# Copies of the first activation chunk at another address, and small products of zeros in the down stages

## The chip, the cores and the metric

The kernel runs on one core of a Trainium2 chip. The metric is device time in microseconds (us) of one execution; a kernel's time is the median of its runs. The engines are TensorE (PE, with its weight loads as PEld), VectorE (DVE), ScalarE (ACT), GpSimd (POOL) and SyncE (SP), which issues the DMAs.

## What is computed

A trunk of two layers on 256 tokens of 1024 channels in float32. Each layer is a half-weighted SwiGLU block, a token mixer (stick-breaking attention in layer 0, an RG-LRU recurrent block in layer 1) and another SwiGLU block; each is normalised, scaled and shifted by a conditioning vector, and added to x through a gate.

```
def sublayer_input(x, g, mod_j):
    shift, scale, gate = mod_j[:, 0], mod_j[:, 1], mod_j[:, 2]
    h = rmsnorm(x, g) * (1 + scale[:, None, :]) + shift[:, None, :]
    return h, (1 + gate)[:, None, :]

def swiglu(h, w_gu, w_down):
    g, u = jnp.split(h @ w_gu, 2, axis=-1)
    return (jax.nn.silu(g) * u) @ w_down

# per layer:  x = x + 0.5 * gate * swiglu(h);  x = x + gate * mixer(h);  x = x + 0.5 * gate * swiglu(h)
```

The feed-forward width is 2816, that of the recurrent block 1280.

## The kernel before

The activations stand transposed, channels on the partitions: x is eight chunks (d or k = 0 to 7) of 128 channels x 256 tokens. All large products are of float32 values split in two float32r parts, a high one (wh, and the first tile of a pair hx or arenar) and the rest (wl, and the second). One step of a product is three matmuls of 128 x 128 weights with 128 x 256 moving values, high by high, high by rest and rest by high; they are issued on line 540, in Acc.group.

Weights come by DMA in pieces of 1 MiB (raw, three buffers), ScalarE makes the high part (L511, fh in load) and VectorE the rest (L514, fl). The rings wh and wl have seven tiles each of 128 x 1024.

A sub-layer has an up stage and a down stage. In the up stage of a feed-forward block there are 22 tiles (f = 0 to 21) of two column blocks (gate and up) each; one tile takes eight chunks k of the normalised input, two halves g and three passes, 48 products in all, into one bank of PSUM. In up, chunk k is read from hx_[k], a pair of tiles of the ring hx (20 places, 384 floats apart, 256 or 258 of them used). After it, swiglu_tile makes the result and splits it into a pair in the arena (arenar). The down stage multiplies these with wdn, eight output chunks d by 22 steps, 528 products; its accumulators are five banks. The residual is added at its end (L674), with the squares for the next norm (L609), and scaled makes a first input for the next sub-layer that isn't divided by the root mean square yet (hx, L632 and L634, 258 columns: the last two carry the shift).

With this input the first two tiles of the next sub-layer (NFIRST) are computed in up_first, while norm and norm_chunk make the final input chunk by chunk (VectorE hpre L642, ScalarE hx L490, VectorE hx L644); the tiles from the third on read that. I call this passage a hand-over; there are five. The very first sub-layer has none: its first eight tiles are computed chunk by chunk together (eight wide chunks of 48 products each), and the tiles f = 8 to 21 follow as usual.

The order is not that of the code. Each operation is handed to Program with an engine, a cost and its buffers; schedule works out due times, simulates the engines with these costs, and issues in the order of the simulated starts. A matmul's cost comes from c_mm, that of a step of three products of 256 columns being 3 x 117.8 ns. The rows of modw (144 pieces, products with cact at L572 on VectorE) are handed out by hook along the way; all DMAs are on SP's queue.

Two tiles only shift addresses: pad0 (HXPAD, 112 floats) ahead of the ring hx and pad1 (ARPAD, 16 floats) ahead of the arena.

Of the kernel before, what the change touches and what calls it, by code (L numbers as in the profile page):

```python
# [14 lines left out]
P = 128  # L15
T = 256
# [16 lines left out]
NFIRST = 2  # L33
LAT0 = 950.0
SMALL = (0, 7)
HXPAD, ARPAD = 112, 16

OFF_NG = 0
OFF_MB = OFF_NG + 6 * KD
# [315 lines left out]


def c_mm(n, passes=3):
    return (432.0 if passes == 4 else 117.8 * passes) * max(n, 256) / 256


def c_dma(n):
# [4 lines left out]
def trunk(ctx, tc, xT, cb, par, modw, gu0, gu, wdn, qk, wv, wo, win, wri, wout, out):  # L366
# [24 lines left out]
    whr, _ = ring("wh", 7, HALF, F32R)  # L391
    wlr, _ = ring("wl", 7, HALF, F32R)
    const.tile([P, HXPAD], F32, tag="pad0", name="pad0")
    hxr, _ = ring("hx", 20, TX, F32R, pitch=384)
    sqr, _ = ring("sq", 2, T)
    ssqr, _ = ring("ssq", 2, T)
    rmsr, _ = ring("rms", 1, T)
# [41 lines left out]
    def fixed(name, cols, dt=F32):  # L439
        return const.tile([P, cols], dt, tag=name, name=name)  # L440
# [14 lines left out]
    none_ = fixed("none", P, F32R)  # L455
    dve.tensor_copy(none_, t32[:, P:])
    ident = fixed("ident", P, BF16)
    mask = fixed("mask", T, BF16)
    pool.affine_select(at[1][:, :P], ones, [[1, P]], ALU.is_equal, 0.0, base=0, channel_multiplier=-1)
    dve.tensor_copy(ident, at[1][:, :P])  # L460
# [132 lines left out]
            V(lambda: dve.tensor_scalar(fo(), mi(), 1.0, wt, ALU.add, ALU.mult), n, rr, ww)  # L593


    ssq, hcur, gcur = {}, {}, {}

    def add_square(gen, d):
        if d == 0:
# [47 lines left out]
    def norm(gen, q):  # L647
        for d in range(KD):
            norm_chunk(gen, d, q)

    def down(l, s, nxt, srcs, ys, nlast, hook=None, post=None, n32=0):


        accs = [Acc(f"acc_{l}_{s}_{i}") for i in range(5)]
        place = [(accs[d // 2], d % 2) for d in range(7)] + [(accs[4], 0)]
        gate = mfin[l, s, 2]
        n = len(srcs)
        ws = []

        def step(d, k):  # L660
            acc, j = place[d]
            y, yc = ys(k)
            o = lambda b: b[:, j * T : (j + 1) * T]
            if k < 2 * n32:
                c0 = (k % 2) * D + d * P
                group32(acc, j, o, ws[k], lambda u: u[:, c0 : c0 + P], y, lambda v: v[:, yc], T, False)
            else:
                group(acc, j, o, ws[k], lambda u: u[:, d * P : (d + 1) * P], y, lambda v: v[:, yc], T, k == 2 * n - 1)

        def residual(d):  # L670
            acc, j = place[d]

            def fn():
                dve.scalar_tensor_tensor(x[d](), acc.b()[:, j * T : (j + 1) * T], gate()[:, d : d + 1], x[d](), ALU.mult,  # L674
                                         ALU.add)
            V(fn, T, [(acc.b, j), (gate, d), x[d]], [x[d]], ptr=1)
            add_square(nxt, d)
            if nxt != "end":
                scaled(nxt, d)
            else:  # L680
                A(x[d], x[d], AF.Copy, T, [x[d], pars], [x[d]], ptr=1, scale=lambda: col(OFF_FG + d))

        for c in range(n):
            if c < n32:
                raw = Buf(rawr)
                dma(raw, srcs[c], CH, [raw])
                ws += [raw, raw]
            else:
                ws += load(srcs[c], CH, f"dn_{l}_{s}_{c}")
            if hook is not None:  # L690
                hook(c)
            if c < n - nlast:
                for d in range(KD):
                    for k in (2 * c, 2 * c + 1):
                        step(d, k)
            if post is not None:
                post(c)
        for ds in ((0, 1), (2, 3), (4, 5), (6,), (7,)):
            for d in ds:
                for k in range(2 * (n - nlast), 2 * n):  # L700
                    step(d, k)
            for d in ds:
                residual(d)

    def up(acc, ws, hx_):

        for k in range(KD):
            for g in range(2):
                c0 = (k % 4) * 256 + g * P
                group(acc, (g, 0), lambda b, g=g: b[:, g * T : (g + 1) * T], ws[k // 4],  # L710
                      lambda u, c0=c0: u[:, c0 : c0 + P], hx_[k], lambda v: v[:, :T], T, k == KD - 1)

    def up_first(gen, ws, scale=(1.0, 1.0)):

# [35 lines left out]
    def ffn(l, s, nxt, hook):  # L750
# [8 lines left out]
        if j == 0:  # L759
# [32 lines left out]
                              lambda u, c0=c0: u[:, c0 : c0 + P], hcur[0, 0][k], lambda v: v[:, :T], T, k == KD - 1)  # L792
            for f in range(SQ):
                swiglu_tile(accs[f], tile_out())
        else:
            f0 = NFIRST

# [8 lines left out]
        for f in range(f0, NF):  # L806
            hook(f)
            acc = Acc(f"g_{j}_{f}")
            up(acc, load(gu[j, f], CH, f"gu_{j}_{f}", chained if j == 0 and f == f0 else None), hcur[l, s])
            swiglu_tile(acc, tile_out())  # L810
        down(l, s, nxt, [wdn[j, :, 2 * c : 2 * c + 2, :].rearrange("p k d -> p (k d)") for c in range(NF // 2)],
             lambda k: (ys[k], slice(0, T)), 2, lambda c: hook(NF + 2 * c))
# [2 lines left out]
    def attention(l, s, nxt, hook):  # L815
# [45 lines left out]
        def q_proj(f):  # L861
# [11 lines left out]
                    put(g, *v)  # L873
                return
            acc = Acc(f"qk{f}")
            up(acc, q_load(f), hcur[l, s])

            def put2(g, scale):
                b, rd = acc.b, (acc.b, (g, 0))
# [115 lines left out]
        def tail(c):  # L995
# [3 lines left out]
            if c == 1:  # L999
                values(7)  # L1000

        down(l, s, nxt, [wo[:, 2 * c : 2 * c + 2, :].rearrange("p k d -> p (k d)") for c in range(4)],
             lambda k: (os_[k], slice(0, T)), 2, lambda c: hook(8 + c), tail)


    def rglru(l, s, nxt):
# [47 lines left out]
        def xb_proj(n2):  # L1054
# [7 lines left out]
                    A(lambda: xb()[:, 4:], t, AF.Identity, T, [t, rd], [xb], ptr=1, bias=c)  # L1062
            else:
                acc = Acc(f"xb{n2}")
                up(acc, load(win[1, n2], CH, f"xb{n2}"), hcur[l, s])

                def evict(e, xb):
                    A(lambda: xb()[:, 4:], lambda: acc.b()[:, e * T : (e + 1) * T], AF.Copy, T, [(acc.b, (e, 0))], [xb],
# [3 lines left out]

        def gate_proj(n2):
            acc = Acc(f"gt{n2}")
            up(acc, load(win[0, n2], CH, f"gt{n2}"), hcur[l, s])
            b = acc.b
            g = gt[n2] = Buf(F, 4)
            A(g, b, AF.Copy, 2 * T, [(b, (0, 0)), (b, (1, 0))], [g], psum=True)
# [51 lines left out]
        for n2 in range(NB):  # L1130
            output(n2)
        down(l, s, nxt, [wout[:, 2 * c : 2 * c + 2, :].rearrange("p k d -> p (k d)") for c in range(NB)],
             lambda k: ys[k], 2, n32=N32)

    def final():
        q = rstd("end")
# [146 lines left out]
```

## Time and profile before

| | us |
|---|---|
| median of 3 runs | 970.75 |
| lowest, highest | 966.33, 980.56 |
| profiled execution, its own time | 976.08 |
| its span in the trace | 974.3 |

The profile is one execution. A group's row gives the union of its busy times, then the mean length of one record. Records of products overlap, as products are pipelined: a record lasts longer than the time to the next one's start. Line 490 is the helper that issues all of ScalarE's activations, so its groups go by tiles.

### The profile page before, as it was taken

The page shows a single profiled execution, that of the slowest core. Times are in us where ns is not written, and L with a number is a line of the kernel's source. Part 1 is how long each engine was busy: PE and PEld are TensorE (multiplying, and loading weights), DVE is VectorE, ACT ScalarE, POOL GpSimd, SP SyncE. Part 2 cuts the span into 40 slices and gives each one's busy share as a digit, 9 for nine tenths or more (in the row PEclk, how much of TensorE's full clock was granted, in tenths as well). Part 3 has the DMA queues.
Part 4 walks back from the last instruction along what each step waited for, and adds up shares of the span by engine and source line. Part 5 has one row for each costly group of instructions (what it writes and reads, how often), then busy time and mean ns, then how long its engine had stood idle before and what let it go on. Part 6 is the DMA issues. An engine that isn't in the chain of part 4 may idle for free.

```text
span 974.3 us, 19720 instructions
## 1 busy us (share of the span) xinstructions
PE 958.5 (98%) x8096; PEld 946.5 (97%) x8096; DVE 795.5 (82%) x1316; ACT 561.0 (58%) x902; POOL 2.2 (0%) x14
## 2 busy tenths in 40 slices
PE   7999999999999999999999999999999999999997
PEld 5999999999999999999999999999999999999996
DVE  7998988898998999999899999544997997555533
ACT  5475444378886854554366444443869785444333
POOL 0000000000000000000000000000000000000000
PEclk9999999999999999999999999999999999999999
DMA  9989999954775499999976999555424737555531
GB/s 340 364 316 352 350 360 348 350 187 174 250 250 206 142 364 360 363 363 384 345 284 248 348 359 352 214 174 182 164 93 168 258 132 260 178 212 179 173 125 44
DMA packets 48332, 251.25 MB, mean 258 GB/s; under 512 B 5489, under 2 KB 6129, under 8 KB 28530
## 3 DMA queue, kind: packets, MB, share of 16 engines
q1 hardware_dynamic: 48242, 249.99, 69.8%
q8 instruction: 63, 1.03, 0.4%
q14 instruction: 27, 0.22, 0.1%
HBM read 248.92 MB, written 1.05 MB: 257 GB/s over the span
## 4 chain that ended last, share of the span: by engine, by line
PE 79%; DVE 9%; DMA 8%; issue 2%; ACT 1%; SPq 0%; DVEq 0%
PE bank L540 72%; DMA rawm<-in_modw 8%; DVE wl L514 3%; DVE rawm L572 2%; PE bank L844 2%; PE bank L1041 1%; PE bank L967 1%; PE bank L557 1%; PE bank L920 1%; DVE hx L644 1%; PE bank L945 1%; DMA raw<-in_gu 1%; DVE hpre L642 1%; PE bank L1184 0%; DVE arenar L748 0%
## 5 line engine op out<-in xcount | busy, mean ns | idle before, releaser
L540 PE MATMUL bank<-hx,wh 128*128 128x256 f32 (+1 forms) x3392 | 598.0, 280 | 3.6 <-ACT hx L490 2.5
L540 PEld LDWEIGHTS bank<-hx,wh 128*128 128x128 f32 x3392 | 520.3, 189 | 7.0 <-ACT hx L490 3.3
L511 ACT ACTIVATE wh<-raw 128x1024 fp32r<-128x1024 f32 (+1 forms) x328 | 336.8, 1045 | 295.5 <-PE bank L540 211.3
L514 DVE TENSOR_TENSOR wl<-raw,wh 128x1024 fp32r<-128x1024 f32 (+1 forms) x328 | 388.5, 1206 | 116.2 <-ACT wh L511 114.8
L540 PE MATMUL bank<-hx,wl 128*128 128x256 f32 (+1 forms) x1696 | 473.6, 279 | 0.0
L540 PEld LDWEIGHTS bank<-hx,wl 128*128 128x128 f32 x1696 | 319.6, 188 | 0.0
L540 PE MATMUL bank<-arenar,wh 128*128 128x256 f32 x1664 | 289.7, 279 | 0.0
L540 PEld LDWEIGHTS bank<-arenar,wh 128*128 128x128 f32 x1664 | 253.7, 189 | 0.1
L540 PE MATMUL bank<-arenar,wl 128*128 128x256 f32 x832 | 231.8, 279 | 0.0
L572 DVE SCALAR_TENSOR_TENSOR rawm<-rawm,cact 128x1024 f32<-128x1024 f32 x144 | 174.9, 1219 | 21.6 <-DMA rawm<-in_modw 20.9
L540 PEld LDWEIGHTS bank<-arenar,wl 128*128 128x128 f32 x832 | 156.5, 188 | 0.0
L490 ACT ACTIVATE arenar<-a 128x256 fp32r<-128x256 f32 x88 | 35.4, 407 | 18.7 <-DVE a L743 14.3
L748 DVE TENSOR_TENSOR arenar<-a,arenar 128x256 fp32r<-128x256 f32 x88 | 36.3, 417 | 1.2 <-ACT arenar L490 1.2
L490 ACT ACTIVATE sg<-bank 128x256 f32<-128x256 f32 x82 | 29.9, 367 | 8.2 <-PE bank L540 8.2
L743 DVE TENSOR_TENSOR a<-bank,sg 128x256 f32<-128x256 f32 x82 | 33.9, 416 | 0.2
L490 ACT ACTIVATE hx<-hpre,mf 128x256 fp32r<-128x256 f32 x48 | 23.3, 501 | 17.3 <-DVE mf L585 13.4
L490 ACT ACTIVATE hx<-x,mf 128x256 fp32r<-128x256 f32 x40 | 18.6, 502 | 23.7 <-DVE x L674 23.7
L674 DVE SCALAR_TENSOR_TENSOR x<-bank,mf,x 128x256 f32<-128x256 f32 x48 | 21.5, 477 | 8.2 <-PE bank L540 8.2
L844 PE MATMUL bank<-wh,hx 128*128 128x256 f32 x128 | 23.2, 279 | 0.0
L642 DVE SCALAR_TENSOR_TENSOR hpre<-x,mf,rst 128x256 f32<-128x256 f32 x48 | 22.0, 479 | 0.9 <-ACT rst L490 0.4
L644 DVE SCALAR_TENSOR_TENSOR hx<-hpre,mf,hx 128x256 fp32r<-128x256 f32 x48 | 22.7, 478 | 0.0
L490 ACT ACTIVATE arenaf<-arenaf 128x768 f32<-128x768 f32 (+1 forms) x31 | 22.0, 738 | 0.4
(97 smaller groups left out, 448.6 us busy)
## 6 DMA issues: line engine op xcount, KB each, us to landing
raw<-in_gu SPq DMA_DIRECT2D x79, 1024.0 KB, 6.1
rawm<-in_modw SPq DMA_DIRECT2D x144, 512.0 KB, 6.3
raw<-in_wdn SPq DMA_DIRECT2D x44, 1024.0 KB, 6.0
raw<-in_win SPq DMA_DIRECT2D x10, 1024.0 KB, 4.8
raw<-in_qk SPq DMA_DIRECT2D x8, 1024.0 KB, 4.8
raw<-in_gu SPq DMA_DIRECT2D x14, 512.0 KB, 5.9
raw<-in_wout SPq DMA_DIRECT2D x5, 1024.0 KB, 5.0
raw<-in_wv SPq DMA_DIRECT2D x4, 1024.0 KB, 5.8
```

The source lines that it names most:

```text
L490: act.activation(o(), i(), f, **{k: (v() if callable(v) else v) for k, v in kw.items()})
L511: act.activation(h()[:, :m], raw()[:, a : a + m], AF.Copy)
L514: dve.tensor_tensor(lo()[:, :m], raw()[:, a : a + m], f32(h()[:, :m]), ALU.subtract)
L540: pe.matmul(o(b()), wc(u()), xc(v()), start=start and n == 0, stop=stop and n == len(passes) - 1, skip_group_check=True)
L557: pr.op("PE", c_mm(n, 4), lambda: pe.matmul(o(b()), wc(w()), xc(x32()), start=start, stop=stop, skip_group_check=True), [w, x32] + ([] if ...
L572: dve.scalar_tensor_tensor(raw(), raw(), 1.0, cact(), ALU.mult, ALU.mult, accum_out=m()[:, t : t + 1])
L642: V(lambda: dve.scalar_tensor_tensor(hp(), x[d](), gs()[:, c], q(), ALU.mult, ALU.mult), T, [x[d], (gs, d), q], [hp], ptr=1)
L644: V(lambda: dve.scalar_tensor_tensor(lo()[:, :T], hp(), sh()[:, c], f32(hi()[:, :T]), ALU.add, ALU.subtract), T, [hp, (sh, d), hi], [lo], ...
L674: dve.scalar_tensor_tensor(x[d](), acc.b()[:, j * T : (j + 1) * T], gate()[:, d : d + 1], x[d](), ALU.mult, ALU.add)
L743: V(lambda: dve.tensor_tensor(a(), b()[:, T:], sg(), ALU.mult), T, [(b, (1, 0)), sg], [a])
L748: V(lambda: dve.tensor_tensor(y[1](), a(), f32(y[0]()), ALU.subtract), n, [a, y[0]], [y[1]])
L844: pe.matmul(o, u()[:, tb * P : (tb + 1) * P], v()[:, c0 : c0 + 256], start=start and n == 0, stop=k == KD - 1 and n == 2, skip_group_check ...
```

## The change

The tiles of hx lie 320 floats apart instead of 384. A new ring hk holds two tiles of 256 columns behind a pad of 16 floats. At the end of norm (and after the wide tiles of the first sub-layer) other_copy copies both parts of chunk 0 into it, the high part on ScalarE and the rest on VectorE. An up tile with kick set reads chunk 0 from these copies and the other seven from hx as before. Kicked are the feed-forward tiles f in 2, 3, 7, 9, 11, 15, 19 (where the tile is computed by up), all qk tiles from the third on, and all xb and gate tiles of the recurrent block that go through up.

In each down stage, at one of its pieces (the first; in the attention and the recurrent block the second), a product of zeros by 64 columns of the identity, in bf16, is added to the first output chunk's accumulator behind that chunk's first step there. ARPAD becomes 64. The planner's cost of a product becomes 114.0 for 117.8.

```diff
-HXPAD, ARPAD = 112, 16
+HXPAD, HKPAD, ARPAD = 112, 16, 64
+KICKS = (2, 3, 7, 9, 11, 15, 19)
...
-    return (432.0 if passes == 4 else 117.8 * passes) * max(n, 256) / 256
+    return (432.0 if passes == 4 else 114.0 * passes) * max(n, 256) / 256
...
-    hxr, _ = ring("hx", 20, TX, F32R, pitch=384)
+    hxr, _ = ring("hx", 20, TX, F32R, pitch=320)
+    const.tile([P, HKPAD], F32, tag="pad2", name="pad2")
+    hkr, _ = ring("hk", 2, T, F32R)
...
+    zero = fixed("zero", P, BF16)
+    pool.memset(zero, 0.0)
...
     def norm(gen, q):
         for d in range(KD):
             norm_chunk(gen, d, q)
+        other_copy(gen)
+
+    def other_copy(gen):
+        hi, lo = hcur[gen][0]
+        h2, l2 = hkick[gen] = Buf(hkr), Buf(hkr)
+        A(h2, lambda: f32(hi()[:, :T]), AF.Copy, T, [hi], [h2])
+        V(lambda: dve.tensor_copy(l2(), f32(lo()[:, :T])), T, [lo], [l2])
...
-    def down(l, s, nxt, srcs, ys, nlast, hook=None, post=None, n32=0):
+    def down(l, s, nxt, srcs, ys, nlast, hook=None, post=None, n32=0, kicks=(0,)):
...
                     for k in (2 * c, 2 * c + 1):
                         step(d, k)
+                        if d == 0 and k == 2 * c and c in kicks:
+                            kick_op(*place[d])
...
-    def up(acc, ws, hx_):
+    def up(acc, ws, gen, kick=False):
...
+                h = hkick[gen] if kick and k == 0 and gen in hkick else hcur[gen][k]
                 group(acc, (g, 0), lambda b, g=g: b[:, g * T : (g + 1) * T], ws[k // 4],
-                      lambda u, c0=c0: u[:, c0 : c0 + P], hx_[k], lambda v: v[:, :T], T, k == KD - 1)
+                      lambda u, c0=c0: u[:, c0 : c0 + P], h, lambda v: v[:, :T], T, k == KD - 1)
+
+    def kick_op(acc, j):
+
+        b = acc.b
+        pr.op("PE", 130.0, lambda: pe.matmul(b()[:, j * T : j * T + 64], zero, ident[:, :64], start=False, stop=False,
+                                             skip_group_check=True), [(b, "start")], [(b, j)])
...
+            other_copy((0, 0))
...
-            up(acc, load(gu[j, f], CH, f"gu_{j}_{f}", chained if j == 0 and f == f0 else None), hcur[l, s])
+            up(acc, load(gu[j, f], CH, f"gu_{j}_{f}", chained if j == 0 and f == f0 else None), (l, s), f in KICKS)
...
-            up(acc, q_load(f), hcur[l, s])
+            up(acc, q_load(f), (l, s), True)
...
-             lambda k: (os_[k], slice(0, T)), 2, lambda c: hook(8 + c), tail)
+             lambda k: (os_[k], slice(0, T)), 2, lambda c: hook(8 + c), tail, kicks=(1,))
...
-                up(acc, load(win[1, n2], CH, f"xb{n2}"), hcur[l, s])
+                up(acc, load(win[1, n2], CH, f"xb{n2}"), (l, s), True)
...
-            up(acc, load(win[0, n2], CH, f"gt{n2}"), hcur[l, s])
+            up(acc, load(win[0, n2], CH, f"gt{n2}"), (l, s), True)
...
-             lambda k: ys[k], 2, n32=N32)
+             lambda k: ys[k], 2, n32=N32, kicks=(N32,))
```

## Rows read from the trace of the kernel before

**Rows 1.** The page: busy times, granted clock in 40 slices, chain by line.

```profile
PE 958.5 (98%) x8096; PEld 946.5 (97%) x8096; DVE 795.5 (82%) x1316; ACT 561.0 (58%) x902; POOL 2.2 (0%) x14
...
PEclk9999999999999999999999999999999999999999
...
PE bank L540 72%; DMA rawm<-in_modw 8%; DVE wl L514 3%; DVE rawm L572 2%; PE bank L844 2%; PE bank L1041 1%; PE bank L967 1%; PE bank L557 1%; PE bank L920 1%; DVE hx L644 1%; PE bank L945 1%; DMA raw<-in_gu 1%; DVE hpre L642 1%; PE bank L1184 0%; DVE arenar L748 0%
```

**Rows 2.** Windows: from:to, length, busy and (records) per engine; clock, DMA share, GB/s.

```profile
49.60:201.80 152.20, 152.20 (x1294) 152.20 (x1294) 135.37 (x218) 76.35 (x121) 0.00 (x0) 1.00 0.93 343
515.90:689.00 173.10, 173.10 (x1472) 173.10 (x1471) 128.62 (x199) 82.67 (x127) 0.00 (x0) 1.00 0.71 260
709.10:714.30 5.20, 5.20 (x46) 5.20 (x46) 5.13 (x11) 3.94 (x9) 0.00 (x0) 1.00 0.00 0
...
732.80:754.90 22.10, 22.10 (x190) 22.10 (x189) 16.04 (x29) 21.97 (x39) 0.00 (x0) 1.00 0.39 146
762.30:784.50 22.20, 22.20 (x191) 22.20 (x190) 20.38 (x40) 14.99 (x31) 0.00 (x0) 1.00 0.67 242
229.30:234.00 4.70, 4.70 (x42) 4.70 (x42) 4.05 (x7) 3.96 (x6) 0.00 (x0) 1.00 0.90 317
```

**Rows 3.** Windows of two other feed-forward stages and of one tile of 258 columns.

```profile
335.80:499.80 164.00, 164.00 (x1449) 164.00 (x1448) 150.84 (x238) 79.92 (x119) 0.00 (x0) 1.00 0.93 353
797.20:964.90 167.70, 167.70 (x1482) 167.70 (x1481) 93.40 (x128) 79.18 (x117) 0.00 (x0) 1.00 0.47 165
...
791.30:796.70 5.40, 5.40 (x47) 5.40 (x46) 5.40 (x12) 5.34 (x9) 0.00 (x0) 1.00 1.00 401
```

**Rows 4.** Groups by line, 50 to 200 us and 340 to 498 us.

```profile
L540 PE MATMUL bank<-hx,wh 128*128 128x256 f32 x509 | 90.0, 281 | 0.0
...
L540 PE MATMUL bank<-hx,wh 128*128 128x256 f32 x590 | 100.3, 276 | 0.0
```

**Rows 5.** The chain that ended last, in order of time: start, length, what.

```profile
48.92 0.41 DVE hx L644
49.37 158.59 PE bank L540 x1343
```

**Rows 6.** Timeline of TensorE near 796.6 us: start, length, line, operands, form, count.

```profile
796.58 0.28 PE L540 MATMUL bank<-hx,wl 128*128 128x258 f32 x1
796.70 0.41 PE L540 MATMUL bank<-hx,wh 128*128 128x256 f32 x2
```

**Rows 7.** Groups by line, forms apart, whole span: nearest operations and counts.

```profile
L540 PE MATMUL bank<-hx,wh 128*128 128x256 f32 x3072 | 538.6, 280 | 3.2 <-ACT hx L490 2.5 <-DVE hx L644 0.2
L540 PE MATMUL bank<-hx,wl 128*128 128x256 f32 x1536 | 428.2, 279 | 0.0
...
L490 ACT ACTIVATE arenar<-a 128x256 fp32r<-128x256 f32 x88 | 35.4, 407 | 18.7 <-DVE a L743 14.3 <-DVE a L801 4.4
...
L644 DVE SCALAR_TENSOR_TENSOR hx<-hpre,mf,hx 128x256 fp32r<-128x256 f32 x48 | 22.7, 478 | 0.0
L642 DVE SCALAR_TENSOR_TENSOR hpre<-x,mf,rst 128x256 f32<-128x256 f32 x48 | 22.0, 479 | 0.9 <-ACT rst L490 0.4
...
L465 DVE CAST mask<-a 128x256 bf16<-128x256 f32 x1 | 0.3, 294 | 0.4 <-POOL xb L467 0.4
...
L908 PE MATMUL bank<-mask,ident 128*128 128x256 bf16 x16 | 3.1, 278 | 0.0
...
L947 PE MATMUL bank<-arenar,none 128*128 128x128 f32 x32 | 5.3, 248 | 0.0
```

**Rows 8.** Windows of two hand-overs.

```profile
201.90:214.00 12.10, 12.10 (x101) 12.04 (x100) 11.43 (x27) 10.80 (x24) 0.00 (x0) 1.00 0.62 212
...
499.80:515.70 15.90, 15.07 (x118) 14.26 (x116) 15.72 (x34) 14.29 (x25) 0.00 (x0) 1.00 0.61 233
```

**Rows 9.** Waits of 340 to 498 us and 498 to 518 us: us, times, longest.

```profile
ACT wh L511 <- PE bank L540: 54.6, 32, 3.4
...
PEld bank L540 <- DVE hx L644: 0.9, 3, 0.4
```

## What is predicted, and from what

> **What bounds the kernel now.** I began with the page: TensorE is busy for 98% of the span, its granted clock shows the top digit in every slice, and the chain that ended last runs for 72% through one line, L540, the three products of a split matmul [rows 1]. So the end is set by how closely products follow each other, and a change is worth something only if it alters that spacing or stops TensorE.
>
> The busy time does not tell the spacing, since records overlap. The windows do: a window of length w holds (w + one record's length) / spacing products. In two of the four feed-forward stages this gives (152.2 + 0.281) us / 1294 = 117.8 ns and (173.1 + 0.281) / 1472 = 117.8 ns [rows 2]; in the other two (164.0 + 0.276) / 1449 = 113.4 and (167.7 + 0.276) / 1482 = 113.3 ns [rows 3]; the lengths of one record, 281 and 276 ns, differ in the same sense [rows 4]. [...] I call them the 118 and the 113 pace. Vector and scalar engine are not the cause: in the 113 stage from 340 us the scalar engine still waits 54.6 us for TensorE to free weight tiles [rows 9].
>
> What picks the pace? A stretch at 118 begins at 49.37 us, after TensorE had waited for a late chunk, hx from L644 [rows 5]. The stretch at 113 from 797.2 us begins without any wait: 258-column products at about (5.4 + 0.283) / 47 = 121 ns give way directly to 256-column ones, and these run at 113 [rows 3, 6]. There are three such turns from 258 to 256 columns without a wait (the other two near 331 and 701 us), and all three ended at 113. So a wait can end at the slow pace, while slower products just ahead, without a wait, ended at the quick one. This is what I build on; three cases are thin.
>
> The profiled execution took 976.08 us by the clock, 5.3 us above the median of 970.75. One feed-forward stage at the other pace is 1470 x 4.45 ns = 6.5 us, so the spread of the three runs (14.2 us) looks like two stages that fell differently; the sum below is made against 976.08, and what it saves is a draw that the median run had partly won already.
>
> **The change part by part.**
>
> Addresses. Counted in the order of the allocations (2,048 bytes of scratch, four 32-byte constants, then tiles of whole 512 bytes) the weight tiles begin 128 bytes past a multiple of 512, hx and the arena 64 bytes past one (HXPAD 112 and ARPAD 16 floats). After it, hx steps by 1,280 bytes, so it lies at 64 and 320 in turn (64 still, modulo 256); hk, behind 25,600 bytes and a pad of 64, lies at 128; the arena stays at 64. No row has moving data at 320, nor moving data and weights both at 128: what these products cost is bounded by the three spacings seen, 113.3, 117.8 and 121.
>
> Gain. An up tile that is kicked has six products (k = 0, two halves, three passes) on hk, and then returns to hx. If that acts as the 258-column products did, the rest of the tile runs at 113, and so do the tiles behind it. What is at 118 now, behind a first kick:
> - first feed-forward stage: 1294 products, of which 528 are down (11 chunks x 48) and 766 up, 16 tiles of 48. The first kick is f = 9, so 3 x 48 go off, two wide chunks' and f = 8: 1150 x 4.45 ns = 5.1 us [rows 2].
> - third one: kicked from f = 2, 1472 x 4.45 = 6.55 us [rows 2].
> - attention: two qk tiles like the one at 229.3 us, 2 x 42 x 4.45 = 0.4 us [rows 2].
> - recurrent block: two tiles like the one at 709.1, the 190 from 732.8, the 191 down from 762.3: (92 + 381) x 4.45 = 2.1 us [rows 2].
>
> Together 14.1 us. The two stages at 113 stay as they are.
>
> Copies. Six generations, each with a ScalarE copy of 256 columns (0.41 us, as arenar<-a) and a VectorE copy (between the 0.29 of a cast to 256 columns and the 0.48 of L644) [rows 7]. The first stage's pair has a whole tile to finish in: nothing. The other five stand in the hand-over between two sub-layers, where hx is made chunk by chunk and TensorE uses a chunk in 6 x 0.113 = 0.68 us while VectorE needs 2 x 0.48 (L642 and L644) [rows 7]. In the hand-over at 499.8 the weight loads waited for L644 three times [rows 9]. The first kicked product waits for hk, and all products of its tile are queued behind it; the copies in turn stand ahead of later chunks. Between 0 (VectorE moves a weight subtraction back instead) and 5 x (0.41 + 0.48) = 4.5 us; I take one copy exposed each time, 2.0 us, since one hand-over shows such waits and the one at 201.9 none to speak of.
>
> Kicked products. 4 tiles in the first stage, 7 in each of the other three, 6 qk tiles, 3 xb and 5 gate tiles: 39 x 6 = 234. At 113 they cost nothing more, at 121 they cost 234 x 7.6 = 1.8 us; I take the 118 pace, 1.0 us.
>
> Small bf16 products, one in each of six down stages: 64 columns. Nearest are L947 (128 columns, a record of 0.248 us) and L908 (256 columns of bf16, 0.278 us) [rows 7]; a whole record is the upper end, 6 x 0.28 = 1.7 us, the lower 0. I take 0.1 each, 0.6 us. What they do to the pace is a rival below.
>
> Quicker stages elsewhere. The hand-over after the 113 stage took 15.9 us for 118 products, the one after the first 118 stage 12.1 for 101 [rows 8]: at 12.1 / 101 = 0.120 the 118 would have taken 14.1, so 1.8 us were lost to a VectorE that had fallen behind. A quicker first stage, as full of transfers as the second, may lose the same: 0 to 1.8, I take 0.9. The third stage is not as full (DMA share 0.71 against 0.93) [rows 2, 3]: nothing.
>
> New durations (114.0 for 117.8 per product) change only the planner's order. They can move a weight subtraction past a modulation product or back. No row shows the new order; the 1.8 us of one hand-over bounds it either way, taken as 0. The memset on POOL lies before the first product.
>
> Sum: 976.1 - 14.1 + 2.0 + 1.0 + 0.6 + 0.9 = **966.5 us**. With all unknowns at their lower ends it is 962.0, with the upper ends 971.8; the order moves either by 1.8.
>
> [...] The two paces at one clock show that something does hold products back, but no row shows that it is the address.
>
> **The rivals.**
> *The kick does nothing, or only draws again.* For it: the pace after a wait looks like a draw, and six products may be no more than that. Against it: the three turns without a wait. Doing nothing leaves the copies and small products, 976.1 + 2.6 = 978.7 from this execution and 970.75 + 2.6 = 973.4 from the median one; drawing again gives the same on average. I put it at 975.
> *The small products throw the down stages to the slow pace.* [...] Priced by what the forecast has at 113: 4 x 528 + 191 = 2303 x 4.45 = 10.2 us, so 976.7. Against it: the same step could be the one that ends at 113.
> *The other pitch is slower* (the other side). If half or all chunks at another place run at the 121 of the 258-column tile: 4608 products of 256 columns read hx [rows 7]; all of them at 121 add 4608 x 7.6 = 35 us, 1001.5; half add 17.5, 984.0. It decides from a mean of 118.5 ns on all: (990.2 - 966.5) / 4608 = 5.1 ns over 113.3. Against it: modulo 256 nothing moved.
> *A pace below 113.* No row has one; for 951.3 all 8096 products [rows 1] would need 15.2 / 8096 = 1.9 ns less than in the forecast.
>
> **How the numbers follow.** Forecast 0.55, does nothing or draws again 0.25, down stages slow 0.09, slower pitch 0.07, quicker pace 0.04. The predicted time is 966.5. The range of the forecast alone is 960 to 973.6; to leave out no more than 2 in 10 it must take in the second and third case, and I let it run from 958 to 979, outside of which are the slower pitch, most of the quicker pace, and the edges of the rest. A change under 2% can't be told from none by these measurements: faster by over that is under 951.3, slower over 990.2. Faster: 0.03, from the last case. Slower: 0.06, nearly all of the slower pitch. Within: 0.91.
>
> **What would show it.** The windows of the first and third feed-forward stage should hold about 4% more products per microsecond, from the second up tile of the first and the first ordinary tile of the third on, with records of L540 of 276 instead of 281 ns [rows 4]. If the kick only draws, some tiles after a kick run at 118 until the next kick; if it does nothing, whole stages do. If the small products harm, the pace changes from 113 to 118 at the first group of a down stage. A slower pitch shows as a spacing that alternates between the chunks of one tile. The copies show as waits of TensorE for hk or for late hx in the five hand-overs, over 0.5 us each if I took them too cheap. The prediction is wrong if both stages already fell to 113 by chance in the compared runs of before, if the copies stop TensorE in each hand-over, or if the pace hangs on something else than what runs just ahead.

## The result and the profile after

The changed kernel takes 964.3 us (median of 20 runs, 962.67 to 971.47), the kernel before beside it 970.09 (20 runs, 963.75 to 980.56): a ratio of 0.9943, 95% interval 0.9919 to 0.9966. So it is faster by 0.6%, and its runs lie closer together (8.8 us from the lowest to the highest, before 16.8). The profiled execution is the slowest of the twenty (971.47 us, span 969.8), which has to be kept in mind below; a second profiled execution of the same program (r0_changed_again, an empty line added) took 964.55 us.

The page after, against [rows 1]: busy times, the chain by line (two rows), then two groups of part 5 with count, busy time, mean length and idle time.

```profile
PE 950.1 (98%) x8102; PEld 937.1 (97%) x8102; DVE 796.6 (82%) x1322; ACT 563.3 (58%) x908; POOL 2.3 (0%) x15
...
PE 71%; DVE 12%; DMA 10%; ACT 3%; issue 2%; SPq 1%; DVEq 0%
PE bank L545 65%; DMA rawm<-in_modw 10%; DVE wl L519 4%; DVE rawm L577 3%; PE bank L866 2%; DVE arenaf L1045 1%; PE bank L989 1%; ACT wh L516 1%; ACT arenaf L495 1%; DMA raw<-in_gu 1%; PE bank L562 1%; PE bank L942 1%; DVE x L686 1%; DVE hx L649 1%; PE bank L967 1%
...
L545 PE MATMUL bank<-hx,wh 128*128 128x256 f32 (+1 forms) x3236 | 564.8, 279 | 3.9 <-ACT hx L495 3.1
...
L545 PE MATMUL bank<-hk,wh 128*128 128x256 f32 x156 | 31.0, 290 | 0.0
```

L545 is L540 of before. TensorE is still the bound, busy for 98% of the span; in the chain VectorE has 12% and DMA 10%, on the page of before 9% and 8%, which fits a quicker TensorE that catches up with them.

Windows of the profile after (the columns of [rows 2]): the first stage ahead of its first kick, between its first and second kick, its down products; the second stage's down products; the whole third stage and most of the fourth.

```profile
51.40:67.70 16.30, 16.30 (x140) 16.30 (x140) 15.92 (x32) 12.56 (x25) 0.00 (x0) 1.00 0.86 313
69.40:78.70 9.30, 9.30 (x85) 9.30 (x84) 9.30 (x14) 6.80 (x9) 0.00 (x0) 1.00 0.85 316
139.90:198.70 58.80, 58.80 (x521) 58.80 (x520) 49.03 (x81) 23.92 (x37) 0.00 (x0) 1.00 0.94 353
...
440.20:498.90 58.70, 58.70 (x520) 58.70 (x519) 48.55 (x73) 22.95 (x27) 0.00 (x0) 1.00 0.94 356
516.20:684.90 168.70, 168.70 (x1488) 168.66 (x1487) 137.45 (x219) 82.61 (x129) 0.00 (x0) 1.00 0.80 295
795.60:959.70 164.10, 164.10 (x1448) 164.06 (x1447) 90.43 (x116) 76.98 (x113) 0.00 (x0) 1.00 0.48 167
```

Read them by (length + one record) / count. Ahead of the kick (16.30 + 0.281) / 140 = 118.4, with a count this small 118 give or take one; behind it (9.30 + 0.276) / 85 = 112.7, again 113 within one product; the down products (58.80 + 0.276) / 521 = 113.4. The third stage, at 117.8 in [rows 2], now has (168.70 + 0.276) / 1488 = 113.6, kicks included. The first stage of the changed kernel again, ahead of its first kick and behind its second:

```profile
50.90:67.20 16.30, 16.30 (x141) 16.30 (x140) 15.92 (x32) 13.12 (x26) 0.00 (x0) 1.00 0.86 313
79.60:199.00 119.40, 119.40 (x1054) 119.36 (x1054) 104.96 (x167) 57.12 (x87) 0.00 (x0) 1.00 0.93 351
```

That is (16.30 + 0.281) / 141 = 117.6 and (119.40 + 0.276) / 1054 = 113.5. Here is the turn itself in the profile after, TensorE's timeline at the first kicked tile (start, length, operands, count):

```profile
67.72 0.40 PE L545 MATMUL bank<-hx,wh 128*128 128x256 f32 x2
67.96 0.28 PE L545 MATMUL bank<-hx,wl 128*128 128x256 f32 x1
68.08 0.40 PE L545 MATMUL bank<-hk,wh 128*128 128x256 f32 x2
68.31 0.28 PE L545 MATMUL bank<-hk,wl 128*128 128x256 f32 x1
68.44 0.41 PE L545 MATMUL bank<-hk,wh 128*128 128x256 f32 x2
68.68 0.28 PE L545 MATMUL bank<-hk,wl 128*128 128x256 f32 x1
68.80 0.40 PE L545 MATMUL bank<-hx,wh 128*128 128x256 f32 x2
69.03 0.28 PE L545 MATMUL bank<-hx,wl 128*128 128x256 f32 x1
69.15 0.40 PE L545 MATMUL bank<-hx,wh 128*128 128x256 f32 x2
69.39 0.28 PE L545 MATMUL bank<-hx,wl 128*128 128x256 f32 x1
```

The six products on hk take 68.80 - 68.08 = 0.72 us, 120 each; from the third step behind them on the pace is 113. No wait stands in between.

Where the time went, stage by stage: the spans between the first products of the norms (L616 before, L621 in most others), read from the traces, in us.

| stage | before | after | changed again | no kicks | no small | copies at 64 | few kicks |
|---|---|---|---|---|---|---|---|
| first feed-forward | 199.4 | 197.7 | 195.5 | 199.6 | 195.1 | 197.8 | 194.1 |
| attention | 117.2 | 118.2 | 117.5 | 117.1 | 117.3 | 117.4 | 117.7 |
| second feed-forward | 181.4 | 184.2 | 181.4 | 180.6 | 183.1 | 182.1 | 180.6 |
| third feed-forward | 188.4 | 182.8 | 181.3 | 180.6 | 181.4 | 185.2 | 181.0 |
| recurrent | 95.7 | 94.0 | 94.0 | 94.4 | 93.8 | 94.1 | 94.1 |
| fourth feed-forward | 174.9 | 175.3 | 175.3 | 174.9 | 175.1 | 175.0 | 174.9 |

Between the two profiled executions the third stage gives 5.6, the first and the recurrent one 1.7 each, and 2.8 are given back in the second, 1.0 in the attention. The second stage lost them at its end, in the hand-over. Waits from 498 to 520 us, then windows of the same place:

```profile
PE bank L621 <- DVE ssq L614: 1.5, 1, 1.5
DVE rawm L577 <- DMA rawm<-in_modw: 1.1, 1, 1.1
```

```profile
501.90:508.00 6.10, 4.43 (x30) 3.75 (x29) 6.00 (x15) 5.82 (x12) 0.00 (x0) 1.00 0.21 85
508.00:509.30 1.30, 1.10 (x3) 0.93 (x4) 1.30 (x3) 1.30 (x2) 0.00 (x0) 0.61 0.45 113
509.30:511.80 2.50, 2.50 (x14) 2.50 (x13) 2.50 (x3) 2.45 (x4) 0.00 (x0) 0.52 0.99 390
511.80:514.00 2.20, 2.20 (x20) 2.20 (x20) 2.17 (x7) 2.05 (x6) 0.00 (x0) 1.00 0.86 350
```

VectorE had waited 1.1 us for modulation rows, came late with the squares, and the norm's product stood 1.5 us for it. After these stops the granted clock is 0.52 in a window of 2.5 us: 14 products where the next 2.2 us, at 1.00, hold 20. In the second profiled execution of the same program the longest wait of TensorE there is 0.3 us, and the stage takes 181.4.

The attention gained nothing from its kicks. Of its six kicked tiles one ran at 118 behind its kick, in both profiled executions of the changed kernel; its six products on the copies are parted by other products. In the profile after:

```profile
260.90:265.80 4.90, 4.90 (x44) 4.90 (x43) 4.80 (x8) 4.13 (x7) 0.00 (x0) 1.00 0.89 310
```

(4.90 + 0.281) / 44 = 117.8. So a kick does not turn every tile. The kicked tiles that come in at 113 from an unbroken stream, 23 and 22 in the two profiles, all go on at 113.

### The profile page after: what moved, and what is told of

Its sections match the earlier page's. It is cut to its first block, busy times and chain, and to the rows that moved or that the text cites. A ratio compares the mean times of both kernels' runs of the same rounds, so it can differ in the third digit from the quotient of the medians.

```text
span 969.8 us, 19744 instructions
## 1 busy us (share of the span) xinstructions
PE 950.1 (98%) x8102; PEld 937.1 (97%) x8102; DVE 796.6 (82%) x1322; ACT 563.3 (58%) x908; POOL 2.3 (0%) x15
## 4 chain that ended last, share of the span: by engine, by line
PE 71%; DVE 12%; DMA 10%; ACT 3%; issue 2%; SPq 1%; DVEq 0%
PE bank L545 65%; DMA rawm<-in_modw 10%; DVE wl L519 4%; DVE rawm L577 3%; PE bank L866 2%; DVE arenaf L1045 1%; PE bank L989 1%; ACT wh L516 1%; ACT arenaf L495 1%; DMA raw<-in_gu 1%; PE bank L562 1%; PE bank L942 1%; DVE x L686 1%; DVE hx L649 1%; PE bank L967 1%
## 5 line engine op out<-in xcount | busy, mean ns | idle before, releaser
L545 PE MATMUL bank<-hx,wh 128*128 128x256 f32 (+1 forms) x3236 | 564.8, 279 | 3.9 <-ACT hx L495 3.1
L545 PEld LDWEIGHTS bank<-hx,wh 128*128 128x128 f32 x3236 | 493.7, 189 | 6.6 <-ACT hx L495 3.9
L545 PE MATMUL bank<-hx,wl 128*128 128x256 f32 (+1 forms) x1618 | 449.8, 278 | 0.0
L545 PEld LDWEIGHTS bank<-hx,wl 128*128 128x128 f32 x1618 | 306.1, 189 | 0.0
L545 PE MATMUL bank<-arenar,wh 128*128 128x256 f32 x1664 | 285.0, 277 | 0.0
L545 PEld LDWEIGHTS bank<-arenar,wh 128*128 128x128 f32 x1664 | 250.8, 188 | 0.1
L545 PE MATMUL bank<-arenar,wl 128*128 128x256 f32 x832 | 229.7, 276 | 0.0
L545 PEld LDWEIGHTS bank<-arenar,wl 128*128 128x128 f32 x832 | 156.2, 188 | 0.0
L545 PE MATMUL bank<-hk,wh 128*128 128x256 f32 x156 | 31.0, 290 | 0.0
L545 PEld LDWEIGHTS bank<-hk,wh 128*128 128x128 f32 x156 | 24.0, 188 | 0.5
```

What stands on the lines that cost most here:

```text
L545: pe.matmul(o(b()), wc(u()), xc(v()), start=start and n == 0, stop=stop and n == len(passes) - 1, skip_group_check=True)
```

## The experiments

My theory was that the six products at another address turn the stream to 113. Rivals: that the pitch or the planner's new order did it, that reading any other tile is enough, and that the small products do it. Each kernel is the changed one with the edit shown, unless said otherwise; times are medians, with the kernel before beside them on the same chip. Addresses are counted from the order of the allocations, as in the prediction; no trace shows them. The pads move hx, its copies and the arena by steps of 64 bytes; the weights are never moved.

**Without kicks (e1).**

```diff
-h = hkick[gen] if kick and k == 0 and gen in hkick else hcur[gen][k]
+h = hcur[gen][k]
...
-if d == 0 and k == 2 * c and c in kicks:
+if False:
```

> The changed kernel with the copies, the pitch, the pads and the planner's durations, but no up tile reads the copies and no product of zeros is issued. If the kicks set the pace (my theory), the feed-forward stages again take either pace by chance, 6.5 us each: about 970 us, spread 963 to 980, as before, and a stage that starts at 118 stays there for its 20 tiles. If the pitch of 320 floats or the planner's new order is what helped, it stays at about 964 us with narrow spread and all stages at 113.

Measured: 966.42 us (6 runs, 961.86 to 968.96), before 974.96 (14 runs, 968.01 to 981.33), ratio 0.9912 (0.9877 to 0.9947). Neither theory got this right. Windows of its first, second, third and fourth stage:

```profile
50.40:202.00 151.60, 151.60 (x1290) 151.60 (x1289) 131.99 (x212) 77.38 (x123) 0.00 (x0) 1.00 0.91 337
332.00:500.00 168.00, 168.00 (x1484) 168.00 (x1484) 154.29 (x249) 85.18 (x130) 0.00 (x0) 1.00 0.90 342
512.70:680.50 167.80, 167.80 (x1483) 167.80 (x1482) 136.83 (x219) 84.32 (x131) 0.00 (x0) 1.00 0.80 295
787.80:955.00 167.20, 167.20 (x1478) 167.20 (x1477) 94.10 (x127) 79.77 (x117) 0.00 (x0) 1.00 0.48 165
```

The first stage stays at (151.60 + 0.281) / 1290 = 117.7 through all its tiles, as my theory has it; but the other three run at 113.4 without any kick. In this execution none of their hand-overs has a stop over 0.31 us, and the turn from 258 to 256 columns ends at 113 by itself. So the later stages of this execution needed no kick; the third stage of before, whose weight loads waited three times in the hand-over, 0.9 us together [rows 9], ran at 117.8. By medians, too, most of the gain is here without kicks: 8.5 us under the kernel before, against 11.2 for the kernel below that has them but no small products (e3); the two intervals overlap.

**Copies at 64 instead of 128 (e2).** The small products stay.

```diff
-HXPAD, HKPAD, ARPAD = 112, 16, 64
+HXPAD, HKPAD, ARPAD = 112, 0, 80
...
-    const.tile([P, HKPAD], F32, tag="pad2", name="pad2")
```

> The changed kernel with the copies at 64 bytes past a multiple of 256, as hx lies, instead of 128 (the arena stays where it was). If the address of the copies is what disturbs the stream, the six products on the copies run at the pace in which they come, 113.3 or 117.8 ns, no tile turns from 118 to 113 at a kick, and the up stages take either pace by chance: about 967 to 970 us. If reading another tile is enough, whatever its address, all kicked tiles turn to 113 as in the changed kernel: 964 us.

Measured: 965.7 us (7 runs, 961.85 to 970.87), ratio 0.9909 (0.9876 to 0.9942). The time did not tell the two apart, the trace does. Windows: first stage up (with the kicks f = 9, 11, 15, 19) and down, third stage up and down.

```profile
50.50:140.00 89.50, 89.50 (x762) 89.50 (x761) 80.67 (x126) 50.65 (x81) 0.00 (x0) 1.00 0.92 336
141.20:199.80 58.60, 58.60 (x519) 58.60 (x518) 49.97 (x85) 25.98 (x42) 0.00 (x0) 1.00 0.93 353
516.60:624.00 107.40, 107.40 (x914) 107.40 (x913) 98.67 (x156) 53.46 (x87) 0.00 (x0) 1.00 0.91 332
625.90:684.00 58.10, 58.10 (x515) 58.10 (x514) 34.09 (x48) 24.61 (x35) 0.00 (x0) 1.00 0.64 230
```

Both stretches of up products pass all the kicks in them, four and six, at (89.50 + 0.281) / 762 = 117.8 and 117.8: the copies at 64 do nothing. (The third stage came out of its hand-over at 113 and fell to 118 behind stops of at most 0.11 us at 516 us, ahead of this window.) At the first down step both turn to (58.60 + 0.276) / 519 = 113.4 and 113.4. What stands there is the small product, without any wait:

```profile
140.51 0.28 PE L544 MATMUL bank<-arenar,wl 128*128 128x256 f32 x1
140.63 0.20 PE L730 MATMUL bank<-ident,zero 128*128 128x64 bf16 x1
140.67 0.48 PE L544 MATMUL bank<-arenar,wh 128*128 128x256 f32 x2
```

So the address of the copies matters, and the small product turns a stream from 118 to 113 too, twice of two here; the first stage of e1, which has none, passes the same place at 117.7.

**Without the small products (e3).** `if False:` in place of the condition ahead of kick_op.

> The changed kernel without the six products of zeros. If a down stage keeps the pace that the last up tile had, they are not needed: down stages at 113 all the same, and the time the same or up to 0.7 us shorter (6 times the 0.201 us interval less 0.113 us), 963.5 to 964.5 us. If they are what holds the down stages at 113, some of the 528-product stretches fall to 118, 2.3 us each: 966 to 970 us.

Measured: 963.8 us (6 runs, 962.8 to 966.8), ratio 0.9892 (0.9861 to 0.9924). The down stages came in at 113 and stayed there (113.3, 113.6 and 113.3 ns in windows of the first three); where the kicks have done their work the small products are not needed. Their price by the last stage: 175.28 us between its norms in the changed kernel, 175.14 here, 0.14 us each. The kicked tiles' price is the rest, 175.14 against 174.85 without kicks: 0.29 us for seven, 41 ns each.

**Fewer modulation rows in layer 0 (e4).**

```diff
-rate = {0: (1.5, SQ, 30), 1: (1.5, 0, 9), 2: (1.3, 0, 32), 3: (1.3, 0, 32)}
+rate = {0: (1.0, SQ, 30), 1: (1.5, 0, 9), 2: (0.9, 0, 32), 3: (1.3, 0, 32)}
```

> The changed kernel with fewer modulation rows asked for in the two feed-forward stages of layer 0 (1.0 and 0.9 per tile instead of 1.5 and 1.3), so that more of them come in the third. If what the profile after lost in the hand-overs near 206 and 506 us comes from transfers at 350 GB/s that make VectorE late, the longest stops there (1.1 and 1.75 us) shrink below 0.5 us and the time falls by 1.5 to 3 us, to about 961.5 us. If those stops come from the two copies themselves, they stay and the time is 964 us.

Measured: 967.29 us (8 runs, 966.66 to 968.25), ratio 0.9927 (0.99 to 0.9954): by its median slower than e2 and e3 beside it, which keep the rates, where 961.5 was expected. TensorE has no stop by waiting in the hand-overs near 206 and 506 us, as expected if the rows were their cause, but the changed kernel again has none over 0.3 us there either. Its first stage (194.2 us) came in at 113, so its length says nothing of the rows. The attention took 120.5 where the other runs have 117 to 118: three modulation products in a row, 3.45 us, stand on VectorE at its end, and the shift columns of the next input (L637) come late behind them. Waits of TensorE's weight loads from 312 to 326 us:

```profile
PEld bank L545 <- DVE hx L637: 2.3, 4, 0.7
```

The rows have to be brought somewhere, and there they stopped TensorE more.

**The changed kernel again (r0), and the planner's durations or the pitch alone in the kernel before (e5, e6).**

```diff
-    return (432.0 if passes == 4 else 117.8 * passes) * max(n, 256) / 256
+    return (432.0 if passes == 4 else 114.0 * passes) * max(n, 256) / 256
```

```diff
-    hxr, _ = ring("hx", 20, TX, F32R, pitch=384)
+    hxr, _ = ring("hx", 20, TX, F32R, pitch=320)
```

> The changed kernel once more (one empty line added), beside the next three on the same chip. Both theories: 963 to 966 us, most stages at 113.

> The kernel before with the planner's duration 114.0 for 117.8 and nothing else. If it was the new order that made the runs without kicks faster than before (no wait in the hand-overs, so that the turn from 258 to 256 columns ends at 113), this gives most of it: the hand-over near 500 us has no stop over 0.3 us, the third feed-forward stage runs at 113, and the time is some 966 us. If the pitch did it, stages still fall to 118 by chance and the time is 970 to 975 us.

> The kernel before with the tiles of hx 320 instead of 384 floats apart and nothing else (the arena moves by a multiple of 512 bytes). If the order was the cause, nothing changes: stops in the hand-over near 500 us, third stage by chance, 970 to 975 us. If the pitch did it, stages run at 113 after waits too and the time is some 966 us.

Measured, on one chip with before at 973.4 us (21 runs, 965.11 to 980.23): r0 964.55 (5 runs, 962.62 to 965.17), ratio 0.9902 (0.9867 to 0.9937); e5 970.59 (11 runs, 962.24 to 977.65), 0.9954 (0.9914 to 0.9994); e6 973.85 (11 runs, 965.79 to 981.8), 1.001 (0.9969 to 1.005). The pitch does nothing that these runs can tell, though half of the chunks moved by 256 bytes; it is in this sense that addresses are given modulo 256 below. The new durations alone give about half by the ratios, with an interval that nearly reaches 1, and leave the spread of before, 15 us. In the profiled execution of e5, the slowest of its eleven, a hand-over without a wait did not come: the third stage runs at (168.80 + 0.281) / 1436 = 117.7 behind a stop at the norm.

```profile
PE bank L616 <- DVE ssq L609: 0.9, 1, 0.9
```

```profile
521.20:690.00 168.80, 168.80 (x1436) 168.80 (x1435) 130.43 (x199) 79.27 (x123) 0.00 (x0) 1.00 0.78 284
```

The spread is 2.6 us in the five runs of r0 and 8.8 in the twenty of the changed kernel, against 15 and 16 in the eleven each of e5 and e6; but e1 without kicks has 7.1 in six, so that the kick alone makes it small is not shown.

**Fewer kicks (v1).** Kicks only in the first stage (f = 8, 9, 15) and the recurrent block from its fourth xb tile on, copies only for these, one small product, in the recurrent block.

```diff
-KICKS = (2, 3, 7, 9, 11, 15, 19)
+KICKS = (8, 9, 15)
...
-        other_copy(gen)
+        if gen == (1, 1):
+            other_copy(gen)
...
-(l, s), f in KICKS)
+(l, s), j == 0 and f in KICKS)
...
-            up(acc, q_load(f), (l, s), True)
+            up(acc, q_load(f), (l, s))
```

> The changed kernel with kicks only where a wait comes before: tiles 8, 9 and 15 of the first feed-forward stage, the recurrent block from its fourth xb tile on, one small product in that block's down stage; copies only for these two. If copies in the hand-overs are what stops TensorE there, and the other stages turn to 113 by themselves when the hand-over has no wait, all four feed-forward stages run at 113, the hand-overs near 500 us have no stop over 0.5 us, and the time is 960 to 961.5 us, 3 us under the changed kernel. If the kicks were needed in the later stages, some run at 118: 966 us and more.

Measured, on the chip of r0: 962.54 us (5 runs, 961.04 to 969.1), ratio to before 0.9903 (0.9864 to 0.9942). In the profiled execution all four stages run at 113, as expected (113.5 in the first, 113.3 in the others); its four best runs lie between 961.04 and 965.49, those of r0 between 962.62 and 965.17, but one took 969.1, more than any of r0. Its median is lower by 2 us, its ratio to before is the same: not shown to be better. Its first stage came in at 113, so the first kick had nothing to turn. A later stage that waits in its hand-over has no kick here, which would explain the slow run; no trace of that run shows it.

**The copies at other addresses (e8, e9), all of hx at other addresses (e10, e11).** e8 and e9 are without small products, e10 and e11 without kicks and small products; the arena stays at 64 throughout. The four added lines are, in order, e8 (copies at 0), e9 (copies at 192), e10 (all of hx at 128) and e11 (all of hx at 0); each kernel has one of them.

```diff
-HXPAD, HKPAD, ARPAD = 112, 16, 64
+HXPAD, HKPAD, ARPAD = 112, 48, 32
+HXPAD, HKPAD, ARPAD = 112, 32, 48
+HXPAD, HKPAD, ARPAD = 128, 16, 48
+HXPAD, HKPAD, ARPAD = 96, 16, 80 
```

> The changed kernel without the small products and with the copies at a multiple of 256 bytes instead of 128 past one. If any other address than that of hx disturbs the stream as needed, its kicked tiles turn to 113 as in the changed kernel: 963 to 965 us. If 128 is special, since the weights lie there too, tiles that come in at 118 leave a kick at 118: 966 to 970 us.

> The same with the copies at 192 bytes past a multiple of 256. Any address theory: turns to 113, 963 to 965 us. If only 128 works: 966 to 970 us, and kicked products at the pace in which they come.

> The changed kernel without kicks and small products, with all of hx at 128 bytes past a multiple of 256, the arena where it was. If products whose moving data lie as the weights do are slower for good (the six on the copies average 118 to 119 ns in the profile after), all up stages run at one pace of 118 to 121 ns, the down stages as their entry falls: 4608 products times about 5 ns over the quick pace, 980 to 995 us. If they only disturb at the change of address, the up stages take 113 or 118 as before: 962 to 972 us.

> The same with all of hx at a multiple of 256 bytes. If the two paces belong to the distance of 64 bytes between moving data and weights, another distance has another pace or a single one; a single quick pace would make every kick needless and give 960 us, a slow one 980 us and more. If the address does not matter once it is the same throughout, the paces are 113 and 118 by chance: 962 to 972 us.

Measured, three runs each, before at 975.57 us (5 runs): e8 964.07, ratio 0.9894 (0.9841 to 0.9946); e9 982.66, 1.0107 (1.0034 to 1.0181); e10 996.65, 1.0237 (1.0177 to 1.0298); e11 987.67, 1.0131 (1.0077 to 1.0186).

In e8 every feed-forward stage ran at 113 behind its kicks (113.5 to 113.7 ns), but no stretch came to a kick at 118, so the turn from 118 is not shown for it; one kicked qk tile ran at 118 behind its kick. In e9, slower than either case of its expectation, the first stage came in at 113 and stayed there; the second, third and fourth were thrown to 118 at the hand-over, where the first kicked tile follows the 258-column products, and no kick took them out. Windows of e9, part of its first stage up, second and fourth stage:

```profile
67.00:130.00 63.00, 63.00 (x557) 63.00 (x556) 56.87 (x83) 34.23 (x50) 0.00 (x0) 1.00 0.92 345
...
327.00:500.00 173.00, 173.00 (x1471) 173.00 (x1470) 153.31 (x241) 83.61 (x127) 0.00 (x0) 1.00 0.88 329
...
800.00:965.00 165.00, 165.00 (x1403) 165.00 (x1402) 87.12 (x108) 73.91 (x105) 0.00 (x0) 1.00 0.48 166
```

(63.00 + 0.276) / 557 = 113.6, then (173.00 + 0.281) / 1471 = 117.8 and 117.8, six and five kicked tiles included: here copies at 192 left a stream at the pace that it had, and behind the 258-column products the slow one followed them.

The recurrent block gives the addresses a second test, with more cases. In every execution four of its stretches of up products begin directly behind the float32 products of the block's gates (L1041 before, L1063 in most others). How many of them then run at 113, read from the traces:

| before | durations only | pitch only | no kicks | copies at 64 | copies at 192 | copies at 0 | copies at 128 (after, r0, e3, e4, v1) |
|---|---|---|---|---|---|---|---|
| 1 of 4 | 1 of 4 | 1 of 4 | 1 of 4 | 1 of 4 | 0 of 4 | 4 of 4 | 20 of 20 |

Windows of the last and longest of the four: the changed kernel, e8 and e9.

```profile
728.40:749.00 20.60, 20.60 (x182) 20.60 (x182) 14.56 (x26) 19.53 (x36) 0.00 (x0) 1.00 0.47 177
720.40:741.00 20.60, 20.60 (x183) 20.60 (x182) 14.56 (x26) 19.53 (x36) 0.00 (x0) 1.00 0.47 177
732.30:753.00 20.70, 20.70 (x178) 20.70 (x178) 14.66 (x26) 19.90 (x36) 0.00 (x0) 1.00 0.45 170
```

With the kicked products included they have (20.60 + 0.276) / 182 = 114.7, 114.1 and (20.70 + 0.281) / 178 = 117.9. So in these four stretches copies at 0 did as those at 128 (4 of 4 and 20 of 20).

With all of hx at 128 or at 0 no up stage runs at 113. Windows of e10, first stage up and down, second stage up, third stage down; then of e11, first and second stage up:

```profile
60.00:140.00 80.00, 80.00 (x669) 80.00 (x669) 69.86 (x103) 43.78 (x68) 0.00 (x0) 1.00 0.88 326
147.00:205.00 58.00, 58.00 (x513) 58.00 (x512) 50.13 (x88) 27.76 (x44) 0.00 (x0) 1.00 0.88 337
335.00:450.00 115.00, 115.00 (x961) 115.00 (x960) 103.48 (x169) 58.46 (x94) 0.00 (x0) 1.00 0.87 318
...
641.00:699.00 58.00, 58.00 (x495) 58.00 (x494) 31.14 (x41) 23.55 (x31) 0.00 (x0) 1.00 0.59 207
```

```profile
60.00:140.00 80.00, 80.00 (x669) 80.00 (x668) 70.22 (x104) 43.97 (x67) 0.00 (x0) 1.00 0.91 332
...
335.00:440.00 105.00, 105.00 (x888) 105.00 (x887) 95.94 (x151) 52.90 (x82) 0.00 (x0) 1.00 0.89 328
```

(80.00 + 0.283) / 669 = 120.0 and (115.00 + 0.283) / 961 = 120.0 at 128; 120.0 and (105.00 + 0.28) / 888 = 118.6 at 0. The arena, still at 64, takes both paces at the same granted clock: (58.00 + 0.276) / 513 = 113.6 in the first down stage of e10, (58.00 + 0.281) / 495 = 117.7 in the third, and so in its second and fourth. So each of the last three feed-forward stages of e10 takes 8.7 to 8.8 us more than in e1 (189.4 against 180.6 in the third): 960 up products x (120.0 - 113.3) = 6.4 and 528 down products x 4.45 = 2.3.

## Why the prediction was right, and where not

The time is 2.2 us below the 966.5 forecast and within its range, the direction was right, and the main step held: the two paces are there, a kick turns a stage from 118 to 113 (117.6 to 113.5 ns in the first stage of the changed kernel again), and the first stage turned exactly at f = 9, in both profiled executions of the changed kernel (both came to it at 118). By its steps:

*The gain, 14.1 us.* The 4.45 ns in its terms are 117.8 less 113.35, the mean of 113.4 and 113.3 [rows 2, 3]. Against the profiled execution of before the right size: in the changed kernel again the first stage takes 3.9 us less, the third 7.1, the recurrent block 1.7, 12.7 together, kicks' price included. The 0.4 us of the attention did not come (117.2 before, 117.5 in the changed kernel again). Against the median it is less, as the prediction said, since the median run of before had part of it: 5.8 us.

*What turns the pace* was right in the case and too broad in the reason. The prediction built on slower products just ahead, without a wait. In the hand-overs the copies at 192 follow the same 258-column products as those at 64, 128 and 0, and they alone end at 118 (117.8 ns in three stages of e9; 113.5 to 113.7 in e8, which differs from it in the copies' address alone). So slower products just ahead are not enough; in these runs the address made the difference. Whether it acts through the length of the six products is not shown: those that turned the stream took 120 ns, those at 192 about 118. e10 differs from e1 in its pads alone, and its up products take 120.0 ns where those of e1 take 113.4 or 117.7, so the pace of these products changed with the address of their moving data.

*The later stages* were ascribed to the kick alone. In e1 they turn by themselves, to 113.4, behind hand-overs with no stop over 0.31 us. The 6.55 us of the third stage did come, but e1 has them without a kick: that this term fitted is in part luck. The kick's own share is thus mostly the first stage and some of the recurrent block (94.4 us in e1, 94.0 with kicks), and insurance in the others. Why no hand-over of e1 has waits was not isolated: the pitch does not do it, and the planner's durations alone give about half of the time saved, but the one profile of e5 has a wait there. What could be argued is that its slow first stage left the transfers more time; no run tells this apart from the changed order.

*The copies, 2.0 us,* were too dear: e1 makes all six pairs of copies though no product reads them, v1 makes none in the hand-over ahead of the second stage, and this stage takes 180.64 us in both, so making them cost nothing there. In the changed kernel again (181.35) it takes 0.71 us more than in e1, of which 0.43 are kicks and the small product; 0.3 at most is left for waiting on a hand-over's copies.

*Kicked products, 1.0 us,* were too cheap: 39 tiles x 41 ns = 1.6 us. It isn't only the six on hk (0.71 us from 883.84 us in the profile after, 118 each); the three behind them are slow as well (0.35 us, 117 each). *Small products, 0.6:* 6 x 0.14 = 0.8.

*Quicker stages elsewhere, 0.9 us:* a VectorE that falls behind in a hand-over is there, but its place and size depend on the run. Behind the first stage, where the term put it, the profile after waited 0.8 us for the squares:

```profile
PE bank L621 <- DVE ssq L614: 0.8, 1, 0.8
```

Behind the second, which was to stay as it was, it lost 2.8 us, more than the upper end of 1.8; a part of it lies in the 2.5 us at a granted clock of 0.52, which hold 14 products where the 2.2 us behind them hold 20. The changed kernel again lost nothing in either.

*The rivals.* That the kick only draws again: copies at 64 leave stretches at 118 (e2) while those at 128 turned both that they met, and the kicked tiles that came in at 113 from an unbroken stream all stayed there, which a new draw each time would not give; the one qk tile at 118 is the exception. That small products throw down stages to the slow pace: the reverse, 117.8 to 113.4 ns (e2). That the pitch is slower: not this pitch (e6), but products slowed by their address were there, 120.0 ns for all of hx at another address modulo 256 (e10), where the rival had 121.

What remains open: why there are two paces at 64, why 128, 0 and the small product lead to one of them and 192 to the other, what decides after a wait, and what in e1 besides the durations keeps its hand-overs without waits. The runs show the ends, not the cause.

## What to carry to other kernels

Where TensorE is busy throughout, measure the spacing of products, from counts in windows, stage by stage: busy time hid a loss of 4% here (117.8 for 113.3 ns) that no wait showed. Then vary where the moving data lie modulo 256 bytes; the addresses alone moved this kernel by over 3% (ratios to before of 0.9912 in e1 and 1.0237 in e10). And look at runs, not one profile: the same program, whose stages fall to one pace or the other, differed by 15 us from run to run.

## What the runs showed of the hardware that was not expected

- Products of the same shape at the same granted clock run at 113.3, 117.8 or 118.6 to 120.0 ns, by where their moving data lie modulo 256 bytes (data at 64 had 113.3 or 117.8, in before; at 0, 118.6 or 120.0, in e11; at 128, 120.0, in e10). The weights lay at 128 throughout, so that it is the distance from them is not shown.
- One product of 64 columns in bf16, in an otherwise unbroken stream, changed the spacing of the 500 products behind it from 117.8 to 113.4 ns, in both cases on record (e2).
- A stop of TensorE of 1.5 us in a stretch with several shorter ones was followed by a granted clock of 0.52 in 2.5 us (profile after, 509.3 to 511.8 us).
